# Scores' low-part products on full rows instead of half-row pairs, and new TensorE estimates for the planner

## The chip, the cores and the metric

One core of one Trainium2 chip runs the whole program. The metric is device microseconds from start to end of one execution. TensorE multiplies matrices into PSUM, VectorE and ScalarE evacuate PSUM and do elementwise work, GpSimd does some elementwise work without PSUM, and SyncE only issues DMAs.

## What is computed

Two layers of an encoder over 512 tokens of width 1024, with a modulation by a vector c. Each layer normalises x, projects it, runs two branches (differential attention and a gated delta rule over chunks, forward and backward), gates and merges the two, projects back into x, and then runs an MLP of width 4096. The part that the change touches is the attention's scores: four heads, each with two maps of width 64.

```python
def block(qi):                     # 128 queries of every head
    s = jnp.einsum('bhtqd,bhtkd->bhtqk', qi, k).astype(jnp.float32) * scale   # t = 2 maps, d = 64
    p = jax.nn.softmax(s, axis=-1)
    a = p[:, :, 0] - lam * p[:, :, 1]
    return jnp.einsum('bhqk,bhkd->bhqd', a.astype(v.dtype), v)
```

All of it is wanted at float32 accuracy. The kernel gets there on TensorE's faster float32r format by writing an operand as a high and a low part and adding three products: high by high, high by low and low by high.

## The kernel before

Every operation is first taken down in program order by `Plan.add`, then `Plan.schedule` (L250) puts all of them in one static order, and `Plan.issue` (L400, the instructions carry its line, L417) emits them engine by engine. Each engine therefore runs a fixed list. The scheduler is a greedy list scheduler: for each engine it keeps the ready operations by level (chains first, then evacuations, weights, dense products, the modulation last) and it places the earliest one by estimated times. The estimates are in `cost` (L434), the latencies between two engines in `LAG` (L425). For TensorE `cost` says 107 ns for a transpose (L445), 107 ns for a float32r product of up to 256 columns and n / 2.4 + 2.5 ns above that, so 215.8 ns for 512 columns (L448), and for plain float32 products 4 * max(n, columns of the stationary operand) / 2.4 + 5 ns (L447). For VectorE it says 69 ns + 60 ns for each operand that is a column + n / 0.96, so 1136 ns for 1024 elements. The estimates make the order only; nothing on the chip waits for a time.

Memory is dealt out by the same scheduler. Class F holds 21 tiles of 1024 values a partition (weights raw, high and low, the modulation's rows, q2, k2, qs, kh, and three tiles of each delta-rule head), class Y 56 tiles of 512 values, class B the 8 banks of PSUM. A tile's slot comes free after its last reader.

Around the attention the dense work lies ready as filler: the gates' projections (tile d_g, 768 products of 512 columns in the two layers), ordered after the chains by their level.

`attention(h)` (L1158) loads q and k of a head twice, into the upper and the lower 64 partitions of q2 and k2, each [128, 2 maps, 512 tokens]. ScalarE copies them to float32r (qs, kh). VectorE then replaces half of the rows of qs by q's low part, so that one 128-row product of qs with kh gives high by high and low by high at once. For the third product VectorE writes k's low part (kl, L1175) for map 0 into partitions 0 to 63 and for map 1 into partitions 64 to 127 of one Y tile, where qs has its high part. For each of four blocks of 128 queries there are then four products into two banks (sc): two of 128 rows and 512 columns with kh, and two of 64 rows and 512 columns with kl (L1190), of which one lies in the upper and one in the lower half of the array's rows. The two with kl come after both with kh (`whole`). VectorE's maximum (mxv) waits for the last product into its bank, then come ScalarE's exponential (pr), VectorE's combination of both maps, the transposes (aTp), their copy (aT) and the products with v (po).

Of the kernel before, what the change touches and what calls it, by code (L numbers as in the profile page):

```python
# [28 lines left out]
# columns of the array of vectors  # L29
# [3 lines left out]
# columns of the constant array  # L33
# [31 lines left out]
class Tl:  # L65
    """A tile that gets its memory when its first writer is placed."""
# [14 lines left out]
def _rearrange(a, pat, sizes):  # L81
    """einops' rearrange of a numpy view, for splits, permutations and merges."""
# [27 lines left out]
class View:  # L110
    """A part of a tile: its extent as a numpy view, and the steps that lead to it."""
# [69 lines left out]
class Plan:  # L181
    """Takes down the operations of the kernel in program order, gives them an order by estimated times under the
    limits of memory, and issues them in it."""
# [11 lines left out]
    def add(self, engs, fn, args, kw):  # L195
# [14 lines left out]
        for w, vs in ((False, ins), (True, outs)):  # L210
            for v in vs:
# [5 lines left out]
                if w:  # L217
                    for q, o in t.reads:
                        if o is not op and _overlap(q, r):
                            op.preds[o.seq] = o  # L220
                    # what this write covers needs no edge from later writes
                    t.writes = [e for e in t.writes if e[1] is op or not _inside(e[0], r)]
                    t.reads = [e for e in t.reads if e[1] is op or not _inside(e[0], r)]
                    t.writes.append((r, op))
                else:
                    t.reads.append((r, op))
# [5 lines left out]
        # VectorE and GpSimd take turns at their second port to SBUF  # L232
# [6 lines left out]
    def held(self, blocked, order):  # L239
        """What waits for memory, and what holds it."""  # L240
# [8 lines left out]
    # ------------------------------------------------------------------ order  # L249
    def schedule(self):  # L250
# [19 lines left out]
        def offer(op):  # L270
            """Memory for the op, if there is; then it is a candidate from its earliest time."""
# [42 lines left out]
        while todo:  # L314
# [28 lines left out]
            if e != "sp" and op.key[0] >= 0 and HOLD[int(op.key[0])] is not None:  # L343
                # not in the way of a more pressing operation that is about to be ready
# [6 lines left out]
            # two engines don't read one bank of PSUM at the same time  # L351
# [7 lines left out]
            if e == "pe":  # L359
                # TensorE's clock is halved after a window with little work  # L360
# [5 lines left out]
            if any(max(s, free_at[o]) + d < s + c for o, d in zip(op.eng, op.cost) if o != e and o not in op.tried):  # L366
                # another engine would be done with it earlier
                op.tried.add(e)
                continue
# [29 lines left out]
    # ------------------------------------------------------------------ issue  # L399
# [20 lines left out]
# estimates of times in ns, for the order alone  # L420
# [14 lines left out]
def cost(eng, fn, dst, ins, kw):  # L435
# [7 lines left out]
    if eng == "pe":  # L443
        if fn == "transpose":
            return 107.0  # L445
        if kw["lhsT"].dt == F32:
            return 4 * max(n, kw["lhsT"].shape[-1]) / 2.4 + 5.0  # L447
        return 107.0 if n <= 256 else n / 2.4 + 2.5  # L448
# [20 lines left out]
# the pieces of the two branches of each layer, in order: d projections of the delta rule, a b c its three parts,  # L469
# z its gate; q k v projections of the attention, t its heads  # L470
# [5 lines left out]
def encoder(ctx, tc, a, out):  # L476
# [4 lines left out]
    # who is served first: chains, evacuations of dense blocks, weights, dense products, the modulation  # L481
# [21 lines left out]
    # ---------------------------------------------------------------- constants  # L503
# [32 lines left out]
    # ---------------------------------------------------------------- helpers  # L536
    loads = []

    def chunk(src, name, after=(), level=None, cls="F", grp="", wl=2):
        """A weight block [128, nk, n] of 1024 values a partition, as high and low part: views by k."""  # L540
# [20 lines left out]
    def rsqrt(dst, ss, scale):  # L561
        """dst = (ss * scale + eps) ** -0.5: a first guess from the exponent, three Newton steps."""
# [11 lines left out]
    def sumsq(dst, x, by_act):  # L574
        """dst[:, t] = sum of x[:, t]^2 along the row."""
# [10 lines left out]
    def acc(bank, i, lhsT, rhs, stop, level=CHAIN, after=()):  # L586
        """bank[:, i] += lhsT^T rhs: all products into a bank are one group, from the first to the one with stop."""
# [9 lines left out]
    def square(k, xk, hf):  # L597
        """Sums of squares of half of the tokens over the feature tiles of x: a running sum, the last tile for itself."""
# [9 lines left out]
    # ---------------------------------------------------------------- start  # L608
    # twice silu(c), in all partitions
# [6 lines left out]
    # one over the root mean square of x, token-major, on the diagonals of four matrices  # L616
# [10 lines left out]
    # half of the convolution's and of the delta rule's gains: silu(2 u) = u (tanh(u) + 1)  # L627
    dve.tensor_scalar(out=col(O_CONV, 122), in0=col(O_CONV, 122), scalar1=0.5, scalar2=None, op0=ALU.mult, level=WGT)

    # ---------------------------------------------------------------- modulation  # L630
    def ada(l, g, lv, dlv, grp, after=()):
        """Column g of the modulation: the products of 128 rows of the transposed weight with c, summed along the row."""
# [17 lines left out]
    for l in range(DEPTH):  # L650
# [6 lines left out]
        # nlam = -(e0 - e1 + lam_init)  # L657
# [9 lines left out]
    # ---------------------------------------------------------------- norm of x into h  # L667
    def norm_first():
        """x comes token-major, its products with the diagonals normalised and transposed; the modulation column by column."""
# [44 lines left out]
    # ---------------------------------------------------------------- feature-major dense block  # L714
    def dense(blocks, xh, xl, evac, name, after=(), fresh=False, level=None, first=False, fill=False):
        """blocks of weights [128, nk, n]; evac(m, psum) for each 128 columns; three passes: high.high, high.low, low.high.
        With fresh, by halves of the tokens, for an x whose second half comes later; with first, for an x whose feature
        tiles come one after the other."""
# [14 lines left out]
    def dense_halves(blocks, xh, xl, evac, name, after=()):  # L733
        """Blocks of weights [128, nk, 128], for the first half of the tokens and then for the second; evac(m, psum, half)."""
# [13 lines left out]
    def blocks(name, l, n, o=0):  # L748
        """Blocks o .. o + n - 1 of a weight of layer l."""
# [4 lines left out]
    # ---------------------------------------------------------------- the layers  # L754
    mid = []
    for l in range(DEPTH):
# [3 lines left out]
        # ---- per layer constants  # L760
# [19 lines left out]
        # ================================================= differential attention: q, k, v  # L780
# [3 lines left out]
        def da_dense(kind, j):  # L784
            """Columns of one block of two heads, token-major; two banks of two token tiles."""
# [50 lines left out]
        # ================================================= delta rule: projections  # L836
# [36 lines left out]
        # token-major scalars [128, dir, t, h]  # L873
# [4 lines left out]
        def ba_proj():  # L878
            # the high parts of the weights above the low parts: two passes give all products
# [10 lines left out]
            def evac():  # L890
# [9 lines left out]
                # beta = 1 / (1 + exp(-b))  # L900
# [3 lines left out]
                # g = -exp(A_log) * softplus(a + dt_bias)  # L904
# [4 lines left out]
                # log1p(y) = 2 atanh(y / (2 + y))  # L909
# [20 lines left out]
                # the sums as rows  # L930
# [16 lines left out]
        # ================================================= gated delta rule, one head, both directions  # L947
        # Chunks of 128 tokens. With r = 1/|k|, s = beta r^2, A = strict part of (k.k) decay (k not normalised):
        # V = s (I + A diag(s))^-1 (v / r - e^g k S), which is r v_new, so that S and the outputs use k as it is.
        # (A's diagonal is never read: the inversion of its diagonal blocks reads below the diagonal only.)  # L950
# [450 lines left out]
```

## Time and profile before

| | |
|---|---|
| time, median of 3 runs | 1669.7 us (1669.28 to 1670.86) |
| profiled execution, first to last instruction | 1667.5 us |
| the same, median less span: what lies around the instructions | 2.2 us |
| TensorE busy / VectorE busy / ScalarE busy | 1638.8 / 1142.1 / 757.6 us |
| products with kl | 64, of 64 rows and 512 columns |
| products with kh | 64, of 128 rows and 512 columns |

The profiled execution has no separately measured device time; its span is set beside the median of the runs, and the 2.2 us between them are taken as constant. Two things help in reading the rows. Matmuls overlap: the duration of one is its latency, and what it costs the engine is the distance from its start to the start of the next. And the weight load of a product (PEld) normally lies beside the product before it.

### The profile page before, as it was taken

The page shows a single profiled execution, that of the slowest core. Times are in us where ns is not written, and L with a number is a line of the kernel's source. Part 1 is how long each engine was busy: PE and PEld are TensorE (multiplying, and loading weights), DVE is VectorE, ACT ScalarE, POOL GpSimd, SP SyncE. Part 2 cuts the span into 40 slices and gives each one's busy share as a digit, 9 for nine tenths or more (in the row PEclk, how much of TensorE's full clock was granted, in tenths as well). Part 3 has the DMA queues.
Part 4 walks back from the last instruction along what each step waited for, and adds up shares of the span by engine and source line. Part 5 has one row for each costly group of instructions (what it writes and reads, how often), then busy time and mean ns, then how long its engine had stood idle before and what let it go on. Part 6 is the DMA issues. An engine that isn't in the chain of part 4 may idle for free.

```text
span 1667.5 us, 25355 instructions
## 1 busy us (share of the span) xinstructions
PE 1638.8 (98%) x9456; PEld 1410.4 (85%) x9456; DVE 1142.1 (68%) x2653; ACT 757.6 (45%) x1474; POOL 159.2 (10%) x170
## 2 busy tenths in 40 slices
PE   7999999999999999999999999999999999999998
PEld 5889998878898888888998889768889988888887
DVE  7999797898888983333688987998637743333332
ACT  5653452575356252424557335555424652515150
POOL 0231140000300000000023112100002000000000
PEclk9999999999999999999999999999999999999999
DMA  9332534445667982332443332614244433323311
GB/s 379 133 107 96 189 115 146 120 114 186 226 216 265 340 326 90 102 100 90 134 146 113 135 101 72 151 59 126 76 145 139 137 104 101 99 91 101 99 53 51
DMA packets 96782, 232.47 MB, mean 139 GB/s; under 512 B 26625, under 2 KB 37505, under 8 KB 96658
## 3 DMA queue, kind: packets, MB, share of 16 engines
q1 hardware_dynamic: 96658, 230.84, 41.9%
q8 instruction: 74, 1.21, 0.3%
q14 instruction: 50, 0.41, 0.1%
HBM read 217.66 MB, written 13.14 MB: 138 GB/s over the span
## 4 chain that ended last, share of the span: by engine, by line
PE 83%; DVE 12%; DMA 2%; issue 1%; ACT 1%; POOL 0%; SPq 0%; DVEq 0%; ACTq 0%; POOLq 0%
PE d_m L417 39%; PE d_g L417 7%; PE d_dn L417 5%; PE d_out L417 5%; PE d_da L417 5%; PE d_m1f L417 3%; PE d_brb L417 3%; PE d_bra L417 2%; PE d_z L417 2%; PE px L417 2%; PE pv L417 2%; DVE XA L417 2%; DVE btmp L417 2%; PE po L417 1%; PE pog L417 1%
## 5 line engine op out<-in xcount | busy, mean ns | idle before, releaser
L417 PE MATMUL d_m<-uh,wlo_m 128*128 128x512 f32 (+1 forms) x576 | 210.5, 366 | 0.0
L417 PE MATMUL d_m<-ul,whi_m 128*128 128x512 f32 (+1 forms) x576 | 210.4, 365 | 0.0
L417 PE MATMUL d_m<-uh,whi_m 128*128 128x512 f32 (+1 forms) x576 | 210.4, 366 | 0.0
L417 ACT CAST whi_m<-raw_m 128x1024 fp32r<-128x1024 f32 x128 | 132.6, 1049 | 137.1 <-DVE wlo_m L417 70.1
L417 PE MATMUL d_m<-hh,whi_m 128*128 128x512 f32 x448 | 174.3, 389 | 0.0
L417 PE MATMUL d_m<-hl,whi_m 128*128 128x512 f32 x448 | 174.3, 389 | 0.0
L417 PE MATMUL d_m<-hh,wlo_m 128*128 128x512 f32 x448 | 174.3, 389 | 0.0
L417 DVE TENSOR_TENSOR wlo_m<-raw_m,whi_m 128x1024 fp32r<-128x1024 f32 x128 | 156.3, 1221 | 15.8 <-ACT whi_m L417 15.7
L417 DVE SCALAR_TENSOR_TENSOR xT<-d_m,mod,xT 128x512 f32<-128x512 f32 (+1 forms) x72 | 49.7, 690 | 166.5 <-PE d_m L417 166.4
L417 DVE TENSOR_TENSOR ul<-relu,uh 128x512 fp32r<-128x512 f32 x64 | 44.2, 691 | 162.6 <-ACT uh L417 162.6
L417 ACT ACTIVATE relu<-d_m 128x512 f32<-128x512 f32 x56 | 33.5, 598 | 218.8 <-PE d_m L417 218.8
L417 PEld LDWEIGHTS d_m<-ul,whi_m 128*128 128x128 f32 x576 | 108.6, 189 | 17.6
L417 PEld LDWEIGHTS d_m<-uh,wlo_m 128*128 128x128 f32 x576 | 108.6, 189 | 17.5
L417 PEld LDWEIGHTS d_m<-uh,whi_m 128*128 128x128 f32 x576 | 108.6, 189 | 17.4
L417 DVE SCALAR_TENSOR_TENSOR ada<-ada,cb 128x1024 f32<-128x1024 f32 x96 | 116.4, 1227 | 10.0 <-DMA ada<-in_ada_w_dram 8.4
L417 PE MATMUL d_da<-whi_da,hl 128*128 128x256 f32 x384 | 109.4, 287 | 0.0
L417 PE MATMUL d_da<-whi_da,hh 128*128 128x256 f32 x384 | 109.2, 287 | 0.0
L417 PE MATMUL d_da<-wlo_da,hh 128*128 128x256 f32 x384 | 107.5, 287 | 0.0
L417 PE MATMUL d_g<-hh,whi_g 128*128 128x512 f32 x256 | 103.7, 405 | 0.0
L417 PE MATMUL d_g<-hl,whi_g 128*128 128x512 f32 x256 | 103.1, 403 | 0.0
L417 PE MATMUL d_g<-hh,wlo_g 128*128 128x512 f32 x256 | 102.5, 400 | 0.0
L417 PEld LDWEIGHTS d_m<-hh,wlo_m 128*128 128x128 f32 x448 | 84.1, 188 | 17.5
(289 smaller groups left out, 4087.0 us busy)
## 6 DMA issues: line engine op xcount, KB each, us to landing
raw_m<-in_w_mlp_dram SPq DMA_DIRECT2D x128, 512.0 KB, 3.5
ada<-in_ada_w_dram SPq DMA_DIRECT2D x96, 512.0 KB, 6.2
raw_g<-in_w_g_dram SPq DMA_DIRECT2D x32, 512.0 KB, 5.2
raw_out<-in_w_out_dram SPq DMA_DIRECT2D x32, 512.0 KB, 4.3
raw_dn<-in_w_dn_dram SPq DMA_DIRECT2D x24, 512.0 KB, 6.0
raw_da<-in_w_da_dram SPq DMA_DIRECT2D x24, 512.0 KB, 3.9
raw_z<-in_w_dn_dram SPq DMA_DIRECT2D x8, 512.0 KB, 4.9
gb<-grow SPq DMA_DIRECT2D x16, 256.0 KB, 4.7
```

Of the source, the lines that this page charges most:

```text
L417: op.ins = getattr(eng[op.eng[0]], fn)(*[real(v) for v in op.args], **{k: real(v) for k, v in op.kw.items()})
```

## The change

It has two parts. In `attention` the low part of k is computed for both maps in all 128 partitions, in place over k2 (now read as float32r), by one VectorE instruction of 1024 elements instead of two of 512 elements on 64 partitions. The products with kl then use the same 128-row stationary operand as those with kh, so the product with k's low part covers q's high and low part together. The separate Y tile is gone, and k2 stays occupied until the last score of its head. The rule that both kh products come first is gone as well.

In `cost` the estimates of TensorE are set anew: a transpose 109 ns, a float32r product of up to 256 columns 120 ns, above that n / 2.4 + 14 ns (227.3 ns for 512 columns), and a plain float32 product 4 * max(n, 32) / 2.4 + 9 ns. These numbers enter the order of the whole program, not the attention alone. The rest of the diff is comments taken out.

```diff
@@ cost @@
         if fn == "transpose":
-            return 107.0
+            return 109.0
         if kw["lhsT"].dt == F32:
-            return 4 * max(n, kw["lhsT"].shape[-1]) / 2.4 + 5.0
-        return 107.0 if n <= 256 else n / 2.4 + 2.5
+            return 4 * max(n, 32) / 2.4 + 9.0
+        return 120.0 if n <= 256 else n / 2.4 + 14.0
@@ attention @@
-            kl = Y([P, S], "kl", F32R)
+            kl = k2.bitcast(F32R)
...
             for m in range(2):
-                o_, i_ = slice(64 - 64 * m, 128 - 64 * m), slice(64 * m, 64 * m + 64)
+                o_ = slice(64 - 64 * m, 128 - 64 * m)
                 dve.tensor_tensor(out=qs[o_, m], in0=q2[o_, m], in1=qs[o_, m].bitcast(F32), op=ALU.subtract)
-                dve.tensor_tensor(out=kl[i_], in0=k2[i_, m], in1=kh[i_, m].bitcast(F32), op=ALU.subtract)
+            dve.tensor_tensor(out=kl, in0=k2, in1=kh.bitcast(F32), op=ALU.subtract)
...
-                whole = []
-                for m in range(2):
-                    gate["sc"] = pe.matmul(pss[m], lhsT=qs[:, m, qt * P:(qt + 1) * P], rhs=kh[:, m], start=True, stop=False,
-                                           after=opt("sc"))
-                    whole.append(gate["sc"])
-                for m in range(2):
-                    r = slice(64 * m, 64 * m + 64)
-                    pe.matmul(pss[m], lhsT=qs[r, m, qt * P:(qt + 1) * P], rhs=kl[r], start=False, stop=True, after=whole)
+                for i, kk_ in enumerate((kh, kl)):
+                    for m in range(2):
+                        op = pe.matmul(pss[m], lhsT=qs[:, m, qt * P:(qt + 1) * P], rhs=kk_[:, m], start=i == 0, stop=i == 1,
+                                       after=() if i else opt("sc"))
+                        if not i:
+                            gate["sc"] = op
```

## Rows read from the trace of the kernel before

**Rows 1.** The page: busy time by engine, and TensorE's granted clock in 40 slices.
```profile
PE 1638.8 (98%) x9456; PEld 1410.4 (85%) x9456; DVE 1142.1 (68%) x2653; ACT 757.6 (45%) x1474; POOL 159.2 (10%) x170
PEclk9999999999999999999999999999999999999999
```

**Rows 2.** The page: the chain that ended last, whole span, by engine.
```profile
PE 83%; DVE 12%; DMA 2%; issue 1%; ACT 1%; POOL 0%; SPq 0%; DVEq 0%; ACTq 0%; POOLq 0%
```

**Rows 3.** TensorE's timeline in the MLP: start us, duration us; first and last of 20.
```profile
1399.68 0.39 PE L417 MATMUL d_m<-uh,wlo_m 128*128 128x512 f32 x1
...
1403.99 0.39 PE L417 MATMUL d_m<-hh,whi_m 128*128 128x512 f32 x1
```

**Rows 4.** TensorE's timeline in a projection of 256 columns, first and last of 17.
```profile
848.73 0.28 PE L417 MATMUL d_da<-whi_da,hh 128*128 128x256 f32 x1
...
850.64 0.28 PE L417 MATMUL d_da<-whi_da,hl 128*128 128x256 f32 x1
```

**Rows 5.** The scores' tile: instructions, durations in ns (min/median/max), first and last start.
```profile
L417 PE MATMUL sc<-kh,qs x64: 388/446/504, 310.6 to 1177.0; 128*128 128x512 f32 x64
L417 PE MATMUL sc<-kl,qs x64: 491/498/502, 311.4 to 1177.4; 64*128 64x512 f32 x64
```

**Rows 6.** TensorE's timeline, the last block with kl: a pair.
```profile
1177.02 0.40 PE L417 MATMUL sc<-kh,qs 128*128 128x512 f32 x1
1177.35 0.50 PE L417 MATMUL sc<-kl,qs 64*128 64x512 f32 x2
1177.78 0.50 PE L417 MATMUL d_g<-hl,whi_g 128*128 128x512 f32 x1
1178.12 0.40 PE L417 MATMUL d_g<-hh,wlo_g 128*128 128x512 f32 x1
```

**Rows 7.** TensorE's timeline, the first two blocks with kl: single products.
```profile
311.37 0.50 PE L417 MATMUL sc<-kl,qs 64*128 64x512 f32 x1
311.80 0.50 PE L417 MATMUL d_g<-hl,whi_g 128*128 128x512 f32 x1
312.14 0.40 PE L417 MATMUL d_g<-hh,wlo_g 128*128 128x512 f32 x1
312.47 0.50 PE L417 MATMUL sc<-kl,qs 64*128 64x512 f32 x1
312.89 0.49 PE L417 MATMUL pS<-Vk,tok 128*128 128x128 f32 x2
```

**Rows 8.** TensorE's weight loads around another pair; in brackets the idle time before.
```profile
374.56 0.18 PEld L417 LDWEIGHTS sc<-kl,qs 64*128 64x128 f32 x2 [0.37 <-issue]
374.99 0.19 PEld L417 LDWEIGHTS d_g<-hl,whi_g 128*128 128x128 f32 x1 [0.25 <-issue]
```

**Rows 9.** TensorE's timeline elsewhere: a bank's last product, and float32 behind float32r.
```profile
413.91 0.39 PE L417 MATMUL d_g<-hh,wlo_g 128*128 128x512 f32 x1
414.14 0.39 PE L417 MATMUL d_brb<-ybh,whi_brb 128*128 128x512 f32 x1
...
1071.46 0.48 PE L417 MATMUL d_g<-hh,wlo_g 128*128 128x512 f32 x1
1071.77 1.05 PE L417 MATMUL po<-vt,aT 128*128 128x128 f32 x8
```

**Rows 10.** VectorE: the subtractions for kl, and the same operation at 1024 elements.
```profile
L417 DVE TENSOR_TENSOR kl<-k,kh x16: 661/684/691, 310.4 to 1149.5; 64x512 fp32r<-64x512 f32 x16
L417 DVE TENSOR_TENSOR wlo_m<-raw_m,whi_m 128x1024 fp32r<-128x1024 f32 x128 | 156.3, 1221 | 15.8 <-ACT whi_m L417 15.7
```

**Rows 11.** Busy us (instructions) by engine: both attention stretches, and a part of the second.
```profile
309.00:382.00 73.00, 72.58 (x404) 55.57 (x403) 67.56 (x222) 52.11 (x133) 5.51 (x4) 1.00 0.35 95
1058.00:1179.00 121.00, 115.51 (x712) 90.43 (x711) 109.09 (x328) 69.08 (x168) 7.94 (x14) 1.00 0.33 92
1080.00:1110.00 30.00, 26.19 (x129) 18.74 (x128) 28.21 (x80) 17.11 (x38) 3.07 (x6) 1.00 0.17 54
```

**Rows 12.** TensorE's waits by releaser, whole span: us, times, longest us.
```profile
PE xTp L417 <- DVE diag L417: 6.7, 1, 6.7
PE aTp L417 <- DVE pr L417: 2.7, 3, 1.4
PE sc L417 <- DVE qs L417: 2.2, 3, 1.0
```

**Rows 13.** The chain that ended last from 1049 to 1123 us: start us, us, what.
```profile
1049.77 6.44 DMA k<-kT
1060.65 1.20 DVE mxv L417 x2
1102.04 1.30 DVE mxv L417 x2
```

**Rows 14.** VectorE's timeline, back to back.
```profile
555.33 1.22 DVE L417 SCALAR_TENSOR_TENSOR ada<-ada,cb 128x1024 f32<-128x1024 f32 x1
...
556.47 1.22 DVE L417 SCALAR_TENSOR_TENSOR ada<-ada,cb 128x1024 f32<-128x1024 f32 x1
```

## Prediction

> **What bounds the kernel now.** I read the page's busy times first, then the chain that ended last, then TensorE's timeline, and the waits last. TensorE is busy for 1638.8 of 1667.5 us and its granted clock stands at the upper of its two levels, 2.4 GHz, in every slice [rows 1]. The chain that ended last runs through TensorE for 83% of the span and through VectorE for 12% [rows 2]. So the rule for most of the span is simple: a nanosecond less on TensorE is a nanosecond less in the end. The reader has to see two exceptions. First, a busy TensorE says nothing on how well it is used, since matmuls overlap. A float32r product of 512 columns lasts 389 ns, but from the first to the last of twenty in the MLP are 4.31 us for 19 steps, so one costs 227 ns [rows 3]. At 256 columns it is 1.91 us for 16 steps, 119 ns [rows 4]. Where two starts lie farther apart than that, TensorE has lost time without being shown idle. Second, in the attention of layer 1, from some 1050 to 1123 us, the chain goes through the load of k, 6.44 us, and then mostly through VectorE [rows 13]. There TensorE is busy for 26.2 us of 30 while VectorE is busy for 28.2 [rows 11]. A nanosecond taken from TensorE there may only lengthen a wait.
>
> **Part 1, the products with kl.** There are 64 of them, of 64 rows [rows 5]. In the order as issued they lie in 39 blocks: 25 pairs side by side, and 14 alone because the planner put other work between the two. Rows 7 hold the first blocks and rows 6 the last; the counts and the sums below come from the starts in TensorE's timeline over both attention stretches.
>
> A block costs at three places. Entry: the product before it takes 0.33 us from its start to the block's start, not 0.227 (1177.02 to 1177.35, and 312.14 to 312.47) [rows 6, 7]. Exit: from the block's start to the next product are 0.42 to 0.43 us, whether one or two products lie in it (311.37 to 311.80 for one, 1177.35 to 1177.78 for two) [rows 6, 7]. Tail: the product behind the block has 0.34 us to its successor in place of 0.227 (1177.78 to 1178.12, 311.80 to 312.14) [rows 6, 7]. The weight loads say why. The load for a block doesn't lie beside the product before, it starts with the block, after 0.37 us idle, and the next ordinary load starts only with its own product, after 0.25 us idle [rows 8]. So TensorE runs empty before and behind each block.
>
> The two products of a pair do run together: x2 in one row takes 0.50 us where one takes 498 ns [rows 5, 6]. Here two rules of the Trainium skill speak against each other. The page TensorE: Matmul & The Clock Gate, Part 3, says that products in different row groups run at the same time and gives the span as one product's duration and some 4 ns for each further one; by this alone a pair would cost one distance, and undoing 32 pairs would be a loss of 32 x 0.227 = 7.3 us. The page TensorEngine Tiling (Array Packing), Key Properties, says that a change of the tiling mode drains the engine. The trace agrees with both, 0.50 us for x2 and the empty loads of rows 8, and the drain is the larger.
>
> The sum over the 39 blocks: entry 5.4 us above the ordinary distances (most 0.10, some 0.20 where the product before is itself the tail of another block), exit 16.6 us (39 x 0.427). Together 22.0 us. In their place come 64 products at 227 ns, the distance of any 128-row float32r product that follows another [rows 3], which is 14.5 us. That is 7.5 us less. The tails come on top: 34 blocks have one that isn't already counted as the next entry. Seven of these belong to float32 products, whose neighbour pays a like price in any case (0.31 us in place of 0.227, at 1071.46) [rows 9]; the other 27 x 0.11 us are 3.0 us. So TensorE's own list gets 7.5 + 3.0 = **10.5 us** shorter. Bounds: 7.5 if the tails belong to something else, 11.2 if all 34 vanish.
>
> **Where that counts.** 25 blocks, 19 in layer 0 and 6 late in layer 1, lie where TensorE is busy throughout (72.58 of 73 us in layer 0) [rows 11]; they return their share, 25 x 0.27 = 6.7 us. The other 14 lie between 1059 and 1119 us, where the chain goes through VectorE [rows 13]. The bounds for those are 0 and 14 x 0.27 = 3.8 us. I take half, 1.9 us: the gates' products lie ready as filler, but the order is fixed, and there TensorE stands in front of what VectorE has not done. So 8.6 us of 10.5 arrive.
>
> **Part 1, the rest.** VectorE loses 16 x 684 ns and gains 8 x 1221 ns, 10.9 against 9.8 us [rows 10]; I cost this at nothing, since what it hides behind is TensorE's work, and with that cover gone it would be a gain of 1.1 us. A head's first product with kl now waits for one instruction of 1.22 us, not for one of 0.68 us: between 0 and 8 x 0.54 = 4.3 us in all. Before, its partner waited for the second of the old pair just as long, and the kh products and filler lie ahead of it, so I take 0. The removed `whole` lets kl of map 0 run before kh of map 1; that only adds choice. k2's F slot is held through the whole head where the Y slot of kl is given up. Two heads can be in flight, which is at most two more of 21 F tiles beside 12 of weights. A slot that comes free late shows as a later load, and a load of k that comes late stood in the chain with 6.44 us [rows 13]. Between 0 and that, once; I take 0, since the gates' weights would wait first and are filler themselves.
>
> **Part 2, the estimates.** They remove and add no instruction. They make a new order for the whole program. The old ones had TensorE at 215.8 where it takes 227, and at 107 where it takes 119 [rows 3, 4], so 5 to 10% early, and a pair with kl at two times 215.8 where it takes 0.33 - 0.227 + 0.43 + 0.11, some 0.64 us. VectorE's estimate is right already: 1136 ns against 1.14 us from start to start [rows 14]. So on the chip TensorE came later than planned against VectorE, and VectorE's results were mostly there when TensorE asked. That lateness was cover, and it goes away. On the other side, an order made with the right distances puts the filler where it is needed. All that TensorE now loses to waits is small: the longest is 6.7 us at the start, which no estimate changes, and then 2.7 and 2.2 us for VectorE in the attention [rows 12]. I can't sign this part, and take 0. Its size I take from the second attention stretch, in which TensorE is idle for 121 - 115.5 = 5.5 us and in the first for 0.4 us [rows 11]: a new order may heal one such stretch or make another.
>
> **Sum.** The profiled span is 1667.5 us and the median 1669.7, so 2.2 us lie around it and stay. 1667.5 - 8.6 + 2.2 = **1661.1 us**.
>
> **The rivals.**
> *The new order heals* the stretch at 1050 to 1123 us: the loads of k issue earlier, VectorE's maxima come in time, the other 1.9 us arrive and up to 5.5 us of idle time go. 1661.1 - 1.9 - 4 = some 1655 us (1653 to 1657). For it: that idle time is one late chain, not a lack of work. Against: VectorE is at 94% of that stretch.
> *The cover is lost*: with TensorE planned to its true distance and its drains gone, the first attention stretch becomes what the second is, since VectorE is busy for 67.6 of 73 us there too [rows 11]. One more stretch with 5.5 us of waits gives 1666.6, two give 1672.1. So 1664 to 1673, and it decides from the point where VectorE's list in that stretch is longer than TensorE's 73 - 5 = 68 us, which is where it stands now.
> *The gaps stay* and the overlap goes: the empty time belongs to the last product into a bank that VectorE waits for, or to the change of banks, and not to the 64 rows. Then each block keeps its gaps, and the 25 pairs pay 0.227 us more: +5.7 us, 1675.4 us, slower. Against it: elsewhere a bank's last product is followed by the next bank's first after 0.23 us (413.91 to 414.14) [rows 9], and the gap before a block stands ahead of its first product, which can't know that it ends a group. For it: no 128-row stop product of the scores exists before, so it has not been seen. The first of the two rules above, taken alone, points the same way and gives much the same time (1669.7 + 7.3 us, by the page's figure of 4 ns).
>
> **How the numbers follow.** Forecast (1657 to 1664) 0.52, healed 0.20, cover lost 0.22, gaps stay 0.06. A measurement of this kernel can tell some 0.2% from no change, 3.3 us: the bounds are 1666.4 and 1673.0. Forecast, healed and the lower third of cover lost are faster: 0.52 + 0.20 + 0.06 = 0.78. Of the other 0.16 of cover lost 0.12 lies within the bounds; its end, 0.04, and the gaps, 0.06, are slower: 0.10. The range reaches from the healed order's end, 1653, to the middle of cover lost, 1670; what it leaves out is the end of that case, the gaps, and a new order that heals still more.
>
> **What would show it.** Right: no product of 64 rows is left; the 64 products with kl start 0.227 us before their successors; the products around them have no 0.33 and 0.34; TensorE's weight loads for sc no longer stand idle on issue; the MLP stretches are unchanged at 227 ns. Part 2 shows as other work between the scores, and in TensorE's waits for VectorE in the two attention stretches: less than 5.9 us of idle time there is the healed case, over 11 the lost cover. The prediction is wrong if the kl products keep a distance of 0.3 us and more, if the idle time arises in a stage that the first part doesn't touch, or if a load of k stands in the chain of layer 0 as well.

## The result and the profile after

The changed kernel takes 1719.6 us (median of 4 runs, 1717.2 to 1722.7) against 1669.7 us: a ratio of 1.0298, with an interval of 1.0284 to 1.0313. It is slower by 50 us, where 1661.1 us were forecast. Its profiled execution has a span of 1717.5 us against 1667.5 us, so what lies around the span is still some 2 us (1719.6 less 1717.5), and the loss lies in the span.

The page of the changed kernel: busy times, granted clock, and the chain that ended last by engine.

```profile
PE 1646.3 (96%) x9456; PEld 1425.4 (83%) x9456; DVE 1143.3 (67%) x2646; ACT 756.9 (44%) x1473; POOL 167.1 (10%) x170
...
PEclk9999999998999999999999999999999999999999
...
PE 72%; DVE 18%; DMA 4%; ACT 2%; issue 2%; SPq 1%; POOL 0%; POOLq 0%; DVEq 0%; ACTq 0%
```

Beside [rows 1, 2], TensorE's part of the chain falls from 83 to 72%, and VectorE, DMA and ScalarE take it over; in one slice the granted clock falls below 90%. Busy time tells little: TensorE's 1646.3 us are 7.5 us more than before, although its products cost less now. What it waits for tells more. TensorE's waits in the changed kernel (engine, tile, line, what was waited for: us in total, times, longest us):

```profile
PE d_out L417 <- DVE ml L417: 9.0, 3, 7.5
PE d_out L417 <- ACT mh L417: 8.1, 1, 8.1
...
PE pn L417 <- DMA DT<-scrT: 7.1, 3, 4.6
PE aTp L417 <- DVE pr L417: 5.5, 6, 2.0
PE sc L417 <- ACT kh L417: 5.0, 3, 3.2
PE ogT L417 <- POOL og L417: 4.9, 1, 4.9
PE d_brb L417 <- ACT whi_brb L417: 2.4, 1, 2.4
```

In the kernel before nothing behind the start was longer than 1.7 us, and d_out waited 1.2 us in three pieces:

```profile
PE pn L417 <- DMA DT<-scrT: 2.6, 2, 1.7
...
PE d_out L417 <- DVE ml L417: 1.2, 3, 0.5
```

The two longest waits behind the start now stand before d_out, the projection of the merged branches, which lies behind the attention and has none of the changed products.

**The sum.** I took the start of every product on TensorE and set its distance from the one before against the usual distance of its form. Distances that are at least 350 ns too long, behind the first 25 us: 21 of them with 16.4 us before, 40 with 61.7 us after. That is +45 us. The clock costs some 11 us more (last section), and the products with kl give 5 to 8 us back (4.6 us in e1, 8.1 us from e3 to the changed kernel). So 45 + 11 less 5 to 8 is 48 to 51 of the 50 us.

**Two of the waits in full.** The first is the block of the gates that serves as filler. Its level is 3.5, below all dense products, and its result goes to DRAM and is read back for the merge. The stores of it, one for each layer, in the kernel before and then in the changed one (median duration in ns, first and last start):

```profile
L417 SPq DMA_DIRECT2D sg<-sg x2: 326/335/344, 162.4 to 927.4; - x2
```

```profile
L417 SPq DMA_DIRECT2D sg<-sg x2: 326/326/327, 409.3 to 1306.6; - x2
```

Before, TensorE had computed this block by 162 and 927 us, long before it was wanted. Now it comes last, and TensorE waits out the way through DRAM. The chain of the changed kernel there (start us, us, what):

```profile
1302.35 3.64 PE d_g L417 x16
...
1306.01 0.61 ACT sg L417
...
1306.64 2.00 DMA sg<-sg
...
1308.69 2.54 DMA sga<-sg
...
1311.32 0.70 DVE sga L417
...
1312.13 1.29 POOLq L1394
...
1313.45 0.63 ACT mh L417
...
1314.12 1.95 PE d_out L417 x7
```

From the last d_g to the first d_out are 8.1 us in which TensorE has nothing to do. The second wait is a run of the modulation's rows (ada), which have the lowest level of all. VectorE's timeline in the changed kernel, then one row of GpSimd's:

```profile
468.53 1.76 DVE L417 TENSOR_TENSOR ml<-sg,mh 128x512 fp32r<-128x512 f32 x1
...
470.29 1.21 DVE L417 SCALAR_TENSOR_TENSOR ada<-ada,cb 128x1024 f32<-128x1024 f32 x1
...
479.85 1.23 DVE L417 SCALAR_TENSOR_TENSOR ada<-ada,cb 128x1024 f32<-128x1024 f32 x1 [0.32 <-DVE ada L417]
...
481.35 0.69 DVE L417 TENSOR_TENSOR ml<-sg,mh 128x512 fp32r<-128x512 f32 x1
```

```profile
467.56 2.19 POOL L417 TENSOR_TENSOR sg<-sg 128x512 f32<-128x512 f32 x1 [1.23 <-DVE sg L417]
```

GpSimd is through at 469.75 us, and ScalarE has mh ready at 470.40 us. Yet the last ml of the layer stands in VectorE's fixed list behind nine ada, 470.29 to 481.1 us, and d_out waits 7.54 us for it. VectorE is not late with its work: it does what nobody waits for ahead of what TensorE waits for.

### The profile page after: what moved, and what is told of

It reads as the page before. It is cut to its first block, busy times and chain, and to the rows that moved or that the text cites. A ratio compares the mean times of both kernels' runs of the same rounds, so it can differ in the third digit from the quotient of the medians.

```text
span 1717.5 us, 25384 instructions
## 1 busy us (share of the span) xinstructions
PE 1646.3 (96%) x9456; PEld 1425.4 (83%) x9456; DVE 1143.3 (67%) x2646; ACT 756.9 (44%) x1473; POOL 167.1 (10%) x170
## 4 chain that ended last, share of the span: by engine, by line
PE 72%; DVE 18%; DMA 4%; ACT 2%; issue 2%; SPq 1%; POOL 0%; POOLq 0%; DVEq 0%; ACTq 0%
PE d_m L417 37%; PE d_g L417 5%; PE d_da L417 5%; PE d_out L417 4%; PE d_dn L417 3%; PE d_m1f L417 3%; PE d_brb L417 3%; DVE ada L417 2%; PE d_z L417 2%; DVE btmp L417 2%; DVE XA L417 2%; PE px L417 1%; DVE cacc L417 1%; PE d_bra L417 1%; PE pv L417 1%
```

## The experiments

The theories: **the ratio** (part 2 sets TensorE's estimates to the truth, but leaves the others' as they were, so that TensorE is no longer planned early; its lateness on the chip would then have been the list's cover), **the draw** (any change of an estimate shuffles the list, and this shuffle happened to be bad), and **the form** (the new attention itself, above all k2's slot held through a head, upsets the rest).

**The two parts apart.** e1 is the kernel before with the products on full rows and nothing else; k's low part gets two Y tiles, so that no F slot is held longer. e2 is the changed kernel with the old estimates, e3 the kernel before with the new ones.

```diff
 e1, on the kernel before
-            kl = Y([P, S], "kl", F32R)
+            kl = [Y([P, S], "kl", F32R) for m in range(2)]
...
-                dve.tensor_tensor(out=kl[i_], in0=k2[i_, m], in1=kh[i_, m].bitcast(F32), op=ALU.subtract)
+                dve.tensor_tensor(out=kl[m], in0=k2[:, m], in1=kh[:, m].bitcast(F32), op=ALU.subtract)
...
-                    pe.matmul(pss[m], lhsT=qs[r, m, qt * P:(qt + 1) * P], rhs=kl[r], start=False, stop=True, after=whole)
+                    pe.matmul(pss[m], lhsT=qs[:, m, qt * P:(qt + 1) * P], rhs=kl[m], start=False, stop=True, after=whole)
 e2, on the changed kernel (e3 the reverse, on the kernel before)
-            return 109.0
+            return 107.0
...
-            return 4 * max(n, 32) / 2.4 + 9.0
-        return 120.0 if n <= 256 else n / 2.4 + 14.0
+            return 4 * max(n, kw["lhsT"].shape[-1]) / 2.4 + 5.0
+        return 107.0 if n <= 256 else n / 2.4 + 2.5
```

> The kernel before with the low part of k on 128 rows, in two Y tiles (one a map) in place of one, estimates of before. The order of layer 0 is that of before on every engine and that of layer 1 nearly so (158 of 8672 TensorE operations stand elsewhere). It measures the direct effect alone. Theory A (the new estimates cost the time, the product change saves it): 1659 to 1662 us, no idle weight loads for sc, starts 0.227 us apart. Rival B (the attention's new form costs the time, gaps stay): 1675 us or more.

> The changed kernel with the old estimates: the attention's change alone, with kl in place over k2, and the new order that this gives. Theory A: 1657 to 1668 us, since only the estimates are to blame. Rival B (k2's slot held through the head starves loads): over 1700 us. Rival C (any new order scatters by tens of us, whatever made it): anything from 1655 to 1720 us.

> The kernel before with the new estimates: the half-row pairs stay. Theory A: the changed kernel's 1720 us plus the 8 to 11 us that the products save there, 1725 to 1733 us, with the gates' filler block late in both layers. Rival B: 1670 us. Rival C: anything between.

| | us | ratio to before |
|---|---|---|
| e1, products alone | 1665.0 | 0.9971 (0.9959 to 0.9983) |
| e2, part 1 alone | 1677.5 | 1.0041 (1.0026 to 1.0056) |
| e3, part 2 alone | 1727.8 | 1.0346 (1.0331 to 1.0362) |

Part 2 alone loses 58 us, and has the same two waits before d_out. e3's waits:

```profile
PE d_out L417 <- DVE ml L417: 9.5, 3, 7.5
PE d_out L417 <- ACT mh L417: 8.1, 1, 8.1
```

So the loss comes from the estimates. With the new form of the products it is 8.1 us smaller (1727.8 to 1719.6), but these are two different lists, so this is no clean measure of the form. e2 lies above the range of the first theory, 12.4 us above e1, with the old estimates. e1 is 0.3% faster than the kernel before, 4.6 us, and misses its own forecast by 3 us. Its timeline on TensorE shows the drains gone:

```profile
373.65 0.40 PE L417 MATMUL sc<-kh,qs 128*128 128x512 f32 x1
373.89 0.62 PE L417 MATMUL sc<-kl,qs 128*128 128x512 f32 x2
374.35 0.39 PE L417 MATMUL sc<-kh,qs 128*128 128x512 f32 x1
374.58 0.39 PE L417 MATMUL d_g<-hl,whi_g 128*128 128x512 f32 x1
```

Four distances, from 373.65 to 374.58 us, are 0.93 us, 0.23 each, with no entry, exit or tail as in [rows 6, 7]. The rule that both kh products come first is still in e1, so it was not what made the gaps. Where the 4.6 us come from: by the starts the first layer's attention returns 4.5 us, the second's 0.7 (before the first e1 lies 0.6 us behind). Within the second, e1's lead falls from 3.4 us at 1053 us to 2.9 us at 1145 us and then rises to 4.2 us: the 14 blocks beside VectorE's chain return nothing, the late ones 1.3 us. The windows of 1050 to 1125 us say why, in e1 and then in the kernel before (length, then busy us and count of PE, PEld, DVE, ACT, POOL, granted clock, DMA share, GB/s):

```profile
1050.00:1125.00 75.00, 66.31 (x333) 50.84 (x332) 70.16 (x215) 42.11 (x92) 5.11 (x12) 1.00 0.34 88
```

```profile
1050.00:1125.00 75.00, 69.16 (x341) 50.03 (x340) 70.70 (x209) 41.86 (x88) 6.72 (x13) 1.00 0.38 97
```

TensorE is busy for 2.9 us less there, though part of that is that eight fewer of its instructions fall into the window; VectorE is busy for 70.2 us in place of 70.7. TensorE's listed waits in the window sum to 8.3 us in e1 and 5.7 us before, most of them for VectorE: what TensorE saves becomes a wait.

**The two waits taken away.** e4 puts the filler block at the level of the dense products (3). e5 does that and adds a rule to the planner: VectorE doesn't take an operation that shares its turn with GpSimd while a more pressing one of GpSimd is ready.

```diff
 e4 and e5, on the changed kernel
-    URGENT, EARLY, FILL = -1, 1.2, 3.5
+    URGENT, EARLY, FILL = -1, 1.2, 3
 e5 only, in schedule
+            if op.shared and e == "dve":
+                turn = [x[2].cost[x[2].eng.index("pool")] for x in future["pool"] + [(s, *x) for x in ready["pool"]]
+                        if x[0] <= s + 1 and x[1][0] < op.key[0] and x[2].shared and not x[2].done]
+                if turn and free_at["pool"] <= s:
+                    wait = max(wait, s + min(turn))
```

> The changed kernel with the filler block of the gates (first gate block of each layer, written to DRAM and read back) at the level of the dense products instead of below them. Theory A in its narrow form (the planner sees no hole on TensorE for the lowest level, so the block runs last and its way through DRAM is waited for): the stall of 8.3 us before d_out at 1306 us goes, and most of the chain through the reload in layer 0: 1703 to 1712 us. Rival A2 (the cover is lost everywhere and the block is only one place of many): 1708 to 1713 us, only the 8 us. Rival C: it may land anywhere from 1680 to 1730 us.

> The changed kernel with two rules of the planner mended: VectorE's modulation rows (lowest level) no longer go ahead of a more pressing GpSimd operation at the port that both share, and the filler block has the dense products' level. Theory A (the new estimates let the planner itself put gaps on TensorE: 5.1, 1.4 and 2.7 us at 407 to 418 us, 7.7 at 474 and 8.3 at 1306 us): these 25 us go, 1692 to 1700 us. Theory A2 (lost cover: real waits beyond the plan make up most): 1705 us or more. Rival C (scatter): no telling, 1680 to 1720 us.

e4 takes 1712.5 us (1.0251, 1.0233 to 1.0268), e5 1704.8 us (1.0208, 1.0192 to 1.0223). Each edit does at its place what it should: in e4 the wait for mh of 8.1 us is gone, in e5 also the long one for ml. But the sum moves by 7 and 15 us; e5's first theory had 20 to 28. In e4 a longer run of ada comes before the last ml; in e5 other waits stand at other places. One of e4's waits, then some of e5's (its line numbers are 5 higher):

```profile
PE d_out L417 <- DVE ml L417: 15.8, 4, 13.1
```

```profile
PE sc L422 <- ACT kh L422: 7.0, 3, 4.6
PE pn L422 <- DMA DT<-scrT: 5.3, 2, 4.7
PE d_dn L422 <- DVE wlo_dn L422: 4.7, 2, 3.9
```

The two named waits are thus where a part of the loss shows, not all of it. Distances over 350 ns still sum to 48.6 us in e5 (16.4 before).

These two waits are no lateness of the chip against the plan: they stand in the list itself. By the planner's own estimated times, which follow from the code alone, TensorE's gaps behind the first 25 us are 4 us in the kernel before and 27 us in the changed kernel. Of these, 8.5 and 9.2 us stand before d_out, where the chip shows 7.5 and 8.1 us. e4's list plans 12.5 us there (13.1 on the chip), and e5's plans no such gap and 10 us in all. So the 50 us have two parts: gaps that the new list plans, of which e5 brings some 15 us back, and some 35 us that remain in e5, mostly beyond what its list plans.

**The ratio.** Now TensorE keeps its new estimates and all the others are stretched: e6 by 1.08, e14 by 1.10, e16 by 1.03, each on the changed kernel. e9 does the reverse: TensorE's old estimates, the others by 0.95. e13, e10 and e15 have e1's form of the products with the new estimates and the others by 1.00, 1.08 and 1.10.

```diff
 e6 (in e14 and e16 the DMA times too go by 1.10 and 1.03; e9: 0.95 with the old TensorE estimates)
-DMA_LEAD, DMA_TAIL, DMA_STEP, DMA_DEPTH = 1100.0, 900.0, 475.0, 8
+DMA_LEAD, DMA_TAIL, DMA_STEP, DMA_DEPTH = 1188.0, 972.0, 513.0, 8
...
+OTHERS = 1.08
...
 def lag(a, b):
-    return LAG[a][b]
+    return LAG[a][b] * OTHERS
...
 def cost(eng, fn, dst, ins, kw):
+    return cost0(eng, fn, dst, ins, kw) * (1.0 if eng == "pe" else OTHERS)
...
+def cost0(eng, fn, dst, ins, kw):
```

> The changed kernel with the estimates and latencies of all other engines and of DMAs times 1.08, so that TensorE is again early against them by as much as before, at its own true distances. Theory A with cover as the cause (what counts is the ratio of TensorE's estimates to the others'): the filler comes early in both layers and the waits beyond the plan shrink; 1670 to 1690 us. Rival B (the attention's form): 1715 us or more. Rival C: 1680 to 1720 us.

> The run with the attention's change alone (old TensorE estimates, 1677 us), with the estimates and latencies of all other engines and DMAs times 0.95: none of TensorE's own estimates is new, but its ratio to the others is that of the changed kernel. Theory A (the ratio counts, not the truth of a number): the filler late in layer 1, the rows of the modulation ahead of the chain in layer 0; 1700 to 1725 us. Rival D (the new TensorE numbers themselves, by their shares among TensorE's operations): 1672 to 1685 us.

> The full-row products with kl in two Y tiles, TensorE's new estimates, all other engines' estimates and latencies times 1.08. By the planner's own times it has 9 us less of gaps than the run with the scaled others and kl in place, which took 1679 us. Theory A: 1668 to 1676 us. If gaps of the plan don't come on the chip: 1679 us.

> The kernel before with its 64 products on full rows, k's low part in two Y tiles of its own (as in e1), and the changed kernel's new TensorE estimates; k2 is given up as early as before. Theory of the ratio: the place of k's low part matters little, the new ratio does, so 1700 to 1728 us like the others at this ratio. Rival, k2 held too long: two pairs so far had the form in place 8.7 and 12.4 us slower than this one; if that is the form's price this one lies 9 to 12 us under the changed kernel, 1707 to 1711. Rival, the form in place is the cause: 1665 to 1675.

> The changed kernel with the estimates and latencies of all other engines and of the DMAs times 1.10 instead of 1.08 (e6). TensorE is then planned as early against the rest as in the kernel before, or a little earlier. The planner's own list holds more gaps on TensorE than that of the changed kernel (42 against 36 us). Theory of the ratio: 1670 to 1690. Rival, it is the draw, and what the planner itself leaves as gaps comes out on the chip: 1700 to 1725.

> e13's kernel (two Y tiles, new estimates) with all others times 1.10. The planner's own list holds 43 us of gaps on TensorE. Theory of the ratio: 1665 to 1690. Rival, the draw: 1700 to 1725. Beside e14 it is a third pair of the two forms at one set of estimates: if holding k2 costs 9 to 12 us, it lies that much under e14.

> The changed kernel with all others times 1.03, a ratio between that of the changed kernel (1.00) and e6 (1.08). The planner's own list holds 35 us of gaps, as e6's and the changed kernel's do. Theory of the ratio, if the cover is lost by degrees: between the two, 1685 to 1710. If it is lost at one point: near 1679 or near 1720. Rival, the draw: anywhere from 1670 to 1725, the ratio tells nothing.

| TensorE's estimates, the others by | k2 in place: us, ratio | two Y tiles: us, ratio | distances over 350 ns, k2 in place |
|---|---|---|---|
| old, 0.95 | e9: 1707.2, 1.0215 (1.0200 to 1.0230) | | |
| new, 1.00 | changed kernel: 1719.6, 1.0298 | e13: 1717.6, 1.0278 (1.0262 to 1.0293) | 61.7 us |
| new, 1.03 | e16: 1704.1, 1.0198 (1.0183 to 1.0214) | | 52.0 us |
| new, 1.08 | e6: 1678.7, 1.0057 (1.0042 to 1.0072) | e10: 1670.0, 0.9996 (0.9987 to 1.0005) | 27.6 us |
| new, 1.10 | e14: 1686.7, 1.0096 (1.0079 to 1.0113) | e15: 1688.5, 1.0104 (1.0089 to 1.0119) | 34.9 us |

With the new TensorE estimates untouched, 41 of the 50 us come back when the rest is stretched by 8%, and 16 by 3%; at 10% it is 33. e9 lowers the others without touching TensorE's figures and loses 30 us against e2. e6's list still plans 23 us of gaps, but in stretched times: of 4.1 us before d_out the chip shows 2.2. That is what cover looks like, the others being done sooner than planned. The store of the filler block moves with it. In e6:

```profile
L417 SPq DMA_DIRECT2D sg<-sg x2: 337/380/423, 163.8 to 928.5; - x2
```

and the windows over the largest waits, in the changed kernel and then in e6 (columns as above):

```profile
400.00:425.00 25.00, 16.60 (x93) 13.82 (x93) 22.96 (x64) 14.62 (x34) 3.13 (x3) 0.73 0.60 234
460.00:490.00 30.00, 21.03 (x142) 19.62 (x141) 29.56 (x47) 9.57 (x14) 6.07 (x4) 0.89 0.72 259
1300.00:1320.00 20.00, 11.86 (x62) 10.49 (x61) 8.79 (x10) 5.03 (x8) 5.42 (x4) 0.83 0.30 106
```

```profile
400.00:425.00 25.00, 25.00 (x113) 20.67 (x113) 19.41 (x30) 6.38 (x7) 0.85 (x1) 1.00 0.76 260
460.00:490.00 30.00, 30.00 (x252) 30.00 (x252) 29.23 (x65) 20.52 (x37) 0.00 (x0) 1.00 0.63 222
1300.00:1320.00 20.00, 20.00 (x170) 20.00 (x169) 17.65 (x46) 14.54 (x29) 0.00 (x0) 1.00 0.46 167
```

The windows hold the same times, not the same work. In the second row both kernels are mostly in d_out of layer 0; in the third e6 is in d_out of layer 1, which the changed kernel only begins at 1314.12 us. TensorE has 62 to 142 products in these windows in the changed kernel, 170 to 252 and no idle time in e6.

In e16, between the two, the waits before d_out are still there; in e14 the one for mh is not among the long ones, and that for ml is down to 3.9 us:

```profile
PE d_out L417 <- DVE ml L417: 16.6, 3, 14.6
PE d_out L417 <- ACT mh L417: 8.3, 1, 8.3
```

```profile
PE d_dn L417 <- DVE wlo_dn L417: 5.9, 2, 3.0
PE d_out L417 <- DVE ml L417: 4.8, 3, 3.9
```

The form is not the cause: with the new estimates and k2 given up early, e13 loses as much as the changed kernel. Nor has holding k2 a price that can be told: in place less two tiles is +12.4 us (e2 - e1), +8.7 (e6 - e10), -1.8 (e14 - e15), +2.0 (changed kernel - e13).

**The draw.** e7 raises the estimate of a 512-column product in the kernel before by 0.5 ns, e11 lowers it in e1 by 0.2 ns. e8 and e12 split part 2: e8 has the new estimate for the wide float32r products only, e12 for those up to 256 columns only.

```diff
 e7, on the kernel before
-        return 107.0 if n <= 256 else n / 2.4 + 2.5
+        return 107.0 if n <= 256 else n / 2.4 + 3.0
 e11, on e1
+        return 107.0 if n <= 256 else n / 2.4 + 2.3
 e8, on the changed kernel with e2's old estimates
+        return 107.0 if n <= 256 else n / 2.4 + 14.0
 e12, likewise
+        return 120.0 if n <= 256 else n / 2.4 + 2.5
```

> The kernel before with one estimate moved by 0.5 ns: a float32r product of more than 256 columns at n / 2.4 + 3.0 in place of 2.5. No number can be truer or less true for that. Theory A (size and direction of the estimates matter): 1669 to 1673 us. Rival C (every change of an estimate draws another order, and the one before was a good draw): off by 5 us or more, 1674 to 1690 us.

> The changed kernel with one new estimate only, that of products of more than 256 columns (n / 2.4 + 14); transposes, narrow and float32 products as before. Theory A: this is the estimate with most weight, the filler is late and VectorE's rows go first again; 1710 to 1730 us. If narrow and float32 estimates carry the loss: 1677 to 1690 us, near the run with the attention's change alone.

> The full-row products in two Y tiles with the estimates of before but one: products of more than 256 columns at n / 2.4 + 2.3 in place of 2.5, 0.2 ns less. Rival C (the old estimates stand in a narrow good place, and any step out of it can draw a bad order): the planner itself puts 3.1 and 3.6 us of gaps near 155 us and 13.5 us before the last ml of layer 0 in its list; on the chip 1680 to 1695 us. Theory A without scatter: 1663 to 1668 us, as the run without the step.

> The changed kernel with one new estimate only: 120 ns for products of up to 256 columns. Those of 512 columns, transposes and float32 as before. Theory A: the same two places (filler late, rows of the modulation ahead of the last ml), 1700 to 1715 us. If the narrow estimate carries nothing: 1677 us, as the attention's change alone.

e7: 1673.5 us (1.0022, 1.0012 to 1.0032). e11: 1695.2 us (1.0148, 1.0133 to 1.0163). e8: 1712.8 us (1.0257, 1.0241 to 1.0272). e12: 1701.5 us (1.0187, 1.0170 to 1.0204). e7 lies between its two forecasts, with a change too small to say more. e11's list is 30 us slower than e1's for a fifth of a nanosecond; its waits show another run of ada before the last ml and one new wait early on:

```profile
PE d_out L417 <- DVE ml L417: 13.8, 3, 13.0
...
PE d_z L417 <- DVE wlo_z L417: 6.4, 1, 6.4
```

The 13.0 us before d_out are in e11's own list too, as 13.5. So the draw is real, and no single time here can be laid to the ratio alone. But the groups don't overlap, though they were drawn up with the times known and lie only 6 us apart. Lists in which TensorE is planned as early as before, or nearly (the kernel before, e1, e2, e6, e7, e10, e11, e14, e15), take 1665 to 1695 us. Those with some or all of that taken away (e3, e4, e5, e8, e9, e12, e13, e16 and the changed kernel) take 1702 to 1728. The two waits told in full divide here. In the second group, but for e4 and e5 with their other level, the store of the filler block in layer 1 starts at 1287 to 1314 us in every list, in the first group at 924 to 946 us in every list: that block goes with the ratio. The run of ada before the last ml stands in e11 as well, so a draw alone can make it. Whether half of part 2 is worth 24 or 35 us (e12 and e8 against e2) can't be said from one draw each.

## Why the prediction was wrong

**The products: right in kind, too large in size.** No 64-row product is left, and the drains of [rows 6 to 8] are gone, as e1's rows show. The rival in which the gaps stay falls. The Trainium skill's two rules that were weighed (TensorE: Matmul & The Clock Gate, Part 3; TensorEngine Tiling (Array Packing), Key Properties) come out as the rows had it: the drain is larger than what two products side by side save, and the first rule alone, a loss of 7.3 us, is not what e1 shows. (That figure took 32 pairs; the order had 25 side by side, which makes 5.7 us.) Of the 8.6 us that were to arrive, e1 shows 4.6. What failed in e1 is the 1.9 us taken for half of the 14 blocks beside VectorE's chain: they returned nothing, which was the lower bound. The late blocks of layer 1 gave 1.3 of 1.6 us, and the first layer 4.5 of 19 x 0.27 = 5.1 us.

**k's low part in place: taken at 0, and the runs can't tell another value.** The four pairs above have both signs.

**Part 2: the step that failed.** The prediction said "I can't sign this part, and take 0", with a size of 5.5 us "from the second attention stretch". It measured +58 us without part 1 and +42 us with it (changed kernel less e2). Just ahead of that sentence stood the cause: "That lateness was cover, and it goes away". Two things went wrong behind it. First, the size. The part changes the order of the whole program, and its size was read from the one stretch in which TensorE already waited; that a stretch shows no wait in [rows 12] holds for the old list and says nothing of a new one. Lost cover is not all of it, either: the new list plans 23 us more of gaps than the old one, and that could be worked out from the code without a run. Second, the place. The rival "the cover is lost" was given to the two attention stretches, 1664 to 1673 us. The first of them shows little: in the changed kernel it begins some 15 us later, and in its 73 us TensorE is idle for 2.1 us (columns as above).

```profile
324.00:397.00 73.00, 70.87 (x441) 59.31 (x439) 67.53 (x209) 48.32 (x119) 5.06 (x4) 1.00 0.32 92
```

In the second stretch the waits of aTp for pr grow from 2.7 to 5.5 us, and one of sc for kh has 3.2. The largest ones arose behind the attention, at the merge and d_out. The two of them before d_out are planned gaps. The prediction's own mark for being wrong, idle time "in a stage that the first part doesn't touch", is what the trace shows. What it overlooked is in the code that it had read: the levels. Work of the lowest levels, the filler block and the modulation, is placed only in holes of the plan. In the changed kernel's list the filler block found no hole on TensorE until its result was wanted, and VectorE had one before ml that ada filled. Neither has anything to do with the attention.

**The clock was in no term.** It stands at the upper level in every slice of [rows 1], and the sum took it for granted. In the changed kernel it is at the lower one for some 41 us between 174 and 1318 us, in and behind waits; the products that run in that time lose some 11 us by their distances.

**Still open.** How much of the 50 us is ratio and how much draw: inside one ratio lists lay up to 30 us apart (e1 and e11). That e5's remaining loss is lost cover, spread over many small waits, is argued from e6 and e16 and not shown: each of them has another list, and not each of these waits was traced to its cause.

## What to carry to other kernels

A static list made from estimates depends on their ratio. Correcting one engine's figures alone cost 42 to 58 us here, and stretching the others along brought 41 back; keeping the old order and changing only the instructions was better still (e1, the best version here at 1665.0 us). When an edit touches the planner, its price is that of a new list for the whole program: before a run, compare the gaps that the old and the new list plan, look at the lowest-level work and at who waits behind it, and give the range tens of us to either side, since a step of 0.2 ns was worth 30 us here. Judge an edit of instructions with the order held fixed.

## What the runs showed of the hardware

In the wait of 7.54 us for ml TensorE's clock fell to the lower level, and the products behind it paid too. TensorE's timeline in the changed kernel, after that wait:

```profile
482.69 0.41 PE L417 MATMUL d_out<-ml,whi_out 128*128 128x256 f32 x1
482.90 0.41 PE L417 MATMUL d_out<-mh,wlo_out 128*128 128x256 f32 x1
...
485.03 0.28 PE L417 MATMUL d_out<-ml,whi_out 128*128 128x256 f32 x1
485.15 0.28 PE L417 MATMUL d_out<-mh,wlo_out 128*128 128x256 f32 x1
```

The distance is 0.21 us at first and 0.12 us from 485.03 us on, the 119 ns of [rows 4]: 1.2 and then 2.4 GHz. The granted clock over the windows that hold the long waits is 0.73 to 0.89. So such a wait cost more than its length here; the products at the lower level together make some 11 us of the 50.

VectorE and GpSimd held each other up where they ran side by side on SBUF operands, and the one that started second lasted longer. VectorE's ml lasts 1.76 us at 468.53 us, where GpSimd's sg is under way, and 0.69 us at 481.35 us, alone. That sg, which had started 0.16 us behind VectorE's wlo_out, lasts 2.19 us; with nothing of VectorE beside it, it lasts 1.29 us:

```profile
1286.84 1.29 POOL L417 TENSOR_TENSOR sg<-sg 128x512 f32<-128x512 f32 x1 [56.59 <-DVE sg L417]
```
